# Four-layer trunk on one core: bank order and a fixed order in the convolution's end, the mean on VectorE, first q and k projected together

## The chip, the cores and the metric

The kernel runs on one core of one Trainium2 chip. The metric is the device time of one execution in microseconds; three executions of the kernel before took 1390.39, 1392.49 and 1392.76 us, median 1392.49. Times in the profile are microseconds from the start of the profiled span. Engines: PE is TensorE, PEld its loading of weights, DVE VectorE, ACT ScalarE, POOL GpSimd, SP the engine whose queue issues DMAs.

## The reference, cut to what matters

The input is one sequence of 256 frames with 1024 channels. Four layers follow each other, and each is x += mixer(rms_norm(x)), then x += squared-ReLU MLP(rms_norm(x)) with 4096 hidden channels. The mixers are retention (layers 0 and 3), a convolution module (layer 1) and stick-breaking attention (layer 2). All weights and activations are float32. The change touches these two mixers:

```python
def retention_mixer(xn, w_in, q_gain, k_gain, gn_w, gn_b, w_out):
    q, k, v, g = jnp.split(xn @ w_in, [D_MODEL, 2 * D_MODEL, 4 * D_MODEL], axis=-1)
    q = rms_norm(q.reshape(b, s, RET_HEADS, RET_DK), q_gain)     # 4 heads of 256
    k = rms_norm(k.reshape(b, s, RET_HEADS, RET_DK), k_gain)
    q = apply_rotary(q, s)
    k = apply_rotary(k, s) * (RET_DK ** -0.5)
    ...

def conformer_conv_mixer(xn, pw1_w, pw1_b, dw_w, dw_b, ln_w, ln_b, pw2_w, pw2_b):
    a, gate = jnp.split(xn @ pw1_w + pw1_b, 2, axis=-1)
    h = a * jax.nn.sigmoid(gate)
    h = causal_depthwise_conv(h, dw_w) + dw_b                    # 31 taps, 1024 channels
    h = layer_norm(h, ln_w, ln_b)                                # over the channels
    h = jax.nn.silu(h)
    return h @ pw2_w + pw2_b
```

## The kernel before

Activations lie channel-major: x is four tiles of 128 partitions by two blocks of 256 frames, and a block of 128 channels is called d or k (0 to 7). Products in float32 are made of rounded parts: an activation block z is a tile with a hi half and a lo half side by side (ACT writes hi, L417; DVE writes lo, L418), and each weight unit is split the same way.

**Weights.** 442 units of 128 x 1024 float32, in the order of a list (PLAN), two to a chunk of 1 MB, stream through three buffers (`raw`) by DMAs on SP's queue (L338). Each unit is cast by ACT to `wh` (L350) and DVE subtracts to get `wl` (L351); there are five buffers of each. The buffers `raw` are also used for the shifted copies of the convolution's input (L886).

**Projections.** There are two forms for a pair of 128-column blocks. The wide one (`pair_w`, matmuls at L497 and L498) multiplies `wh` by both halves of z in one matmul of 512 columns, and `wl` by the hi half in one of 256; it needs two PSUM banks, and afterwards the two halves of a bank are summed: two copies on ACT (L516) and two additions on DVE (L517). The narrow one (`pair_b`, L470 to L472) uses three matmuls of 256 columns, one bank, and nothing to sum. PSUM has four banks in the pool `acc` and four in the pool `mis`.

**Retention.** For each head, q and then k are projected with `pair_w`, squared by ACT, scaled, rotated on DVE (L695, L696, L698, L699), and POOL adds the squares of a head's two blocks to a tile. The squares are summed over channels by one matmul for each head on its own group of 32 columns (L704; the trace holds two records for each). The rms of x (`norm_r`) is made beside the first pair. Value projections follow (L857 to L859). At the program's start nine matmuls on ones (L295) keep PE busy while x and the first weights arrive; x, the parameters and pieces of 256 KB of weights alternate on SP's queue.

**Convolution.** Blocks 0 and 1 are convolved on DVE and on ACT with POOL, blocks 2 to 7 on PE by 64 records of small matmuls each (L966) from shifted copies of the input. The results of two blocks share one PSUM bank: 2 and 3, 4 and 5, 6 and 7. DVE takes each block out of PSUM, adding a bias and subtracting a shift (`fin_pe`, L1007), and ACT squares it (L975). Then a matmul adds blocks by column groups (`stats`, L981), four blocks to four groups; ACT copies the result (L1036), eight small matmuls make mean and mean square per frame (L387), DVE copies them (L1043), makes the variance and a reciprocal root by small operations on two columns (L371 to L382), and mean and root are broadcast over partitions by PE and ACT (L394, L398). POOL subtracts the mean from each block (L1054), DVE multiplies by the root (L1062), ACT applies the swish (L1063), and the result is split (L362, L363) for the second pointwise projection, which is 192 narrow matmuls into four banks. A few matmuls on ones (L295) fill PE's waits. DVE then adds the projection to x (L839) and writes the next z (L418) while POOL adds squares (L433).

**Order.** Everywhere but in marked places a scheduler that works when the program is built decides each engine's order. In the convolution the order is written by hand: each step gets a due time from the table TP, the steps are sorted by it, and instructions inside keep that order; weight splits come in between where the scheduler puts them.

## Time and profile before

| | |
|---|---|
| median of three executions | 1392.49 us |
| profiled execution, its own time | 1391.27 us |
| its span | 1389.5 us |
| mean granted TensorE clock | 0.994 |
| busy: PE, PEld, DVE, ACT, POOL | 98 %, 88 %, 71 %, 56 %, 10 % |
| TensorE busy, us | 1367.6 |

The page lists, for the whole span, how busy each engine was and the chain of work that ended last. A timeline row gives the start, the length, the engine, the line, the operation with its tiles, how many instructions were merged, and in brackets for how long the engine had been idle before and what ended that. A windows row gives the busy time of each engine in a stretch. The granted clock is 1.00 at 2.4 GHz and near 0.5 at 1.2 GHz.

### The profile page before, as it was taken

Reading aid. Unit: us, or ns where it says so; the run is one execution under the profiler, and the core shown is the slowest. Engines: PE = TensorE matmul, PEld = TensorE weight load, DVE = VectorE, ACT = ScalarE, POOL = GpSimd, SP = SyncE. Lnnn points to the kernel's source line nnn. Section 1 sums busy time; section 2 is a strip of 40 time slices with the busy share of each in tenths; the row PEclk is TensorE's granted clock in tenths of the full one; section 3 lists DMA queues with packets and bytes.
Section 4 is the critical chain, followed back from the end, with each engine's and each line's share of the span. In section 5 each row is a group of like instructions: output and inputs, shape, how many; then the busy total and the mean of one; then the engine's idle time right before and its main releaser. Section 6 shows DMA issues by size and latency. Waiting matters only on the chain.

```text
span 1389.5 us, 22352 instructions
## 1 busy us (share of the span) xinstructions
PE 1367.6 (98%) x8950; PEld 1218.2 (88%) x8950; DVE 984.6 (71%) x1656; ACT 775.2 (56%) x1165; POOL 145.7 (10%) x133
## 2 busy tenths in 40 slices
PE   8999999999999799999999999999999999999998
PEld 6889999888999388888988898888978999988888
DVE  7976778775678388766578587755587687788643
ACT  6655456664456267654468666644565554555432
POOL 3201003000228020000000010000110010100011
PEclk9999999999999999999999999999999999999999
DMA  7554445555554535555543345555444444555551
GB/s 275 197 179 148 156 152 202 186 189 182 182 183 119 183 122 189 197 189 182 184 180 122 124 168 193 182 189 199 173 167 171 163 148 157 182 183 183 193 191 39
DMA packets 38936, 239.92 MB, mean 173 GB/s; under 512 B 4272, under 2 KB 8752, under 8 KB 11184
## 3 DMA queue, kind: packets, MB, share of 16 engines
q1 hardware_dynamic: 38544, 237.97, 48.8%
q8 instruction: 70, 1.15, 0.3%
q10 hardware_dynamic: 288, 0.52, 0.1%
q14 instruction: 34, 0.28, 0.1%
HBM read 236.54 MB, written 1.93 MB: 172 GB/s over the span
## 4 chain that ended last, share of the span: by engine, by line
PE 95%; DMA 2%; DVE 1%; ACT 1%; issue 0%; SPq 0%; DVEq 0%; ACTq 0%
PE acc L497 33%; PE acc L498 17%; PE acc L470 9%; PE acc L472 9%; PE acc L471 9%; PE acc L857 4%; PE acc L858 4%; PE acc L859 4%; DMA raw<-in_w 2%; PE acc L966 1%; PE mis L387 1%; PE acc L486 1%; PE acc L484 1%; PE acc L485 1%; PE mis L394 1%; DVE wl L351 1%
## 5 line engine op out<-in xcount | busy, mean ns | idle before, releaser
L351 DVE TENSOR_TENSOR wl<-raw,wh 128x1024 fp32r<-128x1024 f32 (+1 forms) x442 | 552.5, 1252 | 299.9 <-ACT wh L350 295.1
L350 ACT CAST wh<-raw 128x1024 fp32r<-128x1024 f32 (+1 forms) x442 | 460.9, 1044 | 436.8 <-PE acc L497 212.1
L497 PE MATMUL acc<-z,wh 128*128 128x512 f32 x1248 | 438.9, 397 | 4.0 <-ACT wh L350 2.1
L498 PE MATMUL acc<-z,wl 128*128 128x256 f32 x1248 | 348.8, 282 | 0.3 <-DVE wl L351 0.3
L497 PEld LDWEIGHTS acc<-z,wh 128*128 128x128 f32 x1248 | 233.9, 189 | 60.5 <-ACT wh L350 3.5
L497 PE MATMUL acc<-big,wh 128*128 128x512 f32 x768 | 267.7, 393 | 0.0
L498 PEld LDWEIGHTS acc<-z,wl 128*128 128x128 f32 x1248 | 236.5, 190 | 3.2 <-DVE wl L351 1.8
L498 PE MATMUL acc<-big,wl 128*128 128x256 f32 x768 | 215.2, 280 | 0.0
L497 PEld LDWEIGHTS acc<-big,wh 128*128 128x128 f32 x768 | 143.8, 187 | 32.7
L472 PE MATMUL acc<-big,wl 128*128 128x256 f32 x576 | 162.3, 283 | 0.0
L471 PE MATMUL acc<-big,wh 128*128 128x256 f32 x576 | 162.3, 283 | 0.0
L470 PE MATMUL acc<-big,wh 128*128 128x256 f32 x576 | 161.5, 284 | 0.0
L498 PEld LDWEIGHTS acc<-big,wl 128*128 128x128 f32 x768 | 145.1, 189 | 0.0
L470 PE MATMUL acc<-z,wh 128*128 128x256 f32 x416 | 118.3, 285 | 0.0
L472 PE MATMUL acc<-z,wl 128*128 128x256 f32 x416 | 118.0, 284 | 0.0
L471 PE MATMUL acc<-z,wh 128*128 128x256 f32 x416 | 117.8, 284 | 0.0
L433 POOL TENSOR_TENSOR t<-t,t 128x512 f32<-128x512 f32 x25 | 38.8, 1554 | 735.1 <-DVE z L418 457.1
L470 PEld LDWEIGHTS acc<-big,wh 128*128 128x128 f32 x576 | 109.5, 192 | 1.3 <-DVE big L362 0.8
L471 PEld LDWEIGHTS acc<-big,wh 128*128 128x128 f32 x576 | 110.4, 192 | 0.1
L472 PEld LDWEIGHTS acc<-big,wl 128*128 128x128 f32 x576 | 110.4, 192 | 0.0
L516 ACT COPY t<-acc 128x256 f32<-128x256 f32 x180 | 65.2, 372 | 56.5 <-PE acc L498 56.5
L857 PE MATMUL acc<-wh,z 128*128 128x512 f32 x224 | 87.9, 394 | 0.0
(232 smaller groups left out, 1807.9 us busy)
## 6 DMA issues: line engine op xcount, KB each, us to landing
raw<-in_w SPq DMA_DIRECT2D x216, 1024.0 KB, 4.8
raw<-hd SPq DMA_DIRECT2D x12, 263.0 KB, 5.3
raw<-in_w SPq DMA_DIRECT2D x6, 512.0 KB, 7.6
x<-in_x SPq DMA_DIRECT2D x4, 256.0 KB, 6.1
raw<-in_w SPq DMA_DIRECT2D x4, 256.0 KB, 7.2
hd<-big SPq DMA_DIRECT2D x6, 143.5 KB, 3.0
cst<-in_cst SPq DMA_DIRECT2D x4, 192.0 KB, 5.0
cst<-in_cst SPq DMA_DIRECT2D x1, 548.0 KB, 8.8
```

The costliest lines, as they stand in the source:

```text
L350: nc.scalar.copy(hi[:, s], src[:, s])
L351: nc.vector.tensor_sub(lo[:, s], src[:, s], hi[:, s])
L433: (nc.vector if p == 3 and self.quick else nc.gpsimd).tensor_add(a, self.sq, q)
L470: nc.tensor.matmul(o, wh[:, kk, cs], ah, start=st, stop=False, **kw)
L471: nc.tensor.matmul(o, wh[:, kk, cs], al, start=False, stop=False, **kw)
L472: nc.tensor.matmul(o, wl[:, kk, cs], ah, start=False, stop=en, **kw)
L497: nc.tensor.matmul(ps[m], wh[:, kk, cs], a, start=first and kk == 0, stop=False, **kw)
L498: nc.tensor.matmul(ps[m][:, :S], wl[:, kk, cs], a[:, :S], start=False, stop=last and kk == 3, **kw)
L516: nc.scalar.copy(o[:, s], ps[m][:, S:])
L857: nc.tensor.matmul(ps[t], zh[:, s], wh[:, kk], start=k == 0, stop=False, skip_group_check=True)
L858: nc.tensor.matmul(ps[t], zh[:, s], wl[:, kk], start=False, stop=False, skip_group_check=True)
L859: nc.tensor.matmul(ps[t], zl[:, s], wh[:, kk], start=False, stop=k == 7, skip_group_check=True)
```

## The change

First layer: `PLAN` gets four units that hold q's and k's weights of the first head side by side, and `pairs_qk` uses two banks of `acc` and two of `mis`, so that each z is multiplied with both. The first weights come in pieces of 512 KB, x in between, and the first four units, not two, are split in halves. The other three heads of layer 0 use the narrow form; layer 3 keeps the wide one. The rms of x in layer 0 is made beside the third head. The four matmuls on the sums of squares are kept together, the last head's first, in both retention layers.

Convolution: blocks 2 to 7 take banks in turn, each bank's second half three blocks later. The due times go; the steps stand in a fixed order. Take-outs, stats, and weight splits are put in order by `issue_after`: the first two splits of the second projection after the take-out of block 5, the rest after the square of block 7 and the third y. The stats by column groups take blocks 0 to 5; blocks 6 and 7 are summed straight to columns. Mean and mean square are read from PSUM. The mean is subtracted on DVE, four blocks at a time, and the swish's input is written in place.

```diff
-                ps = self.pair_w("ret_w_in", j, isk * D + h * DK, self.zs)
+                if j == h == 0:
+                    if not isk:
+                        first = self.pairs_qk("ret_w_in", j, 0)
+                    ps = first[isk]
+                else:
+                    ps = (self.pair_w if j else self.pair_b)("ret_w_in", j, isk * D + h * DK, self.zs)
...
+    def pairs_qk(self, name, l, c0):
+        ps = [[self.acc(), self.acc()], [self.mis(), self.mis()]]
+        for kb in range(4):
+            w = self.unit((name, l, "qk", kb, c0))
+            wh, wl = v3(w[0], 2, 512), v3(w[1], 2, 512)
+            for kk, e in ((0, 0), (0, 1), (1, 0), (1, 1)) if kb < 3 else ((0, 0), (1, 0), (0, 1), (1, 1)):
+                k = kb * 2 + kk
+                z = self.zs(k)
+                for m in range(2):
+                    cs = slice(e * 256 + m * P, e * 256 + (m + 1) * P)
+                    o = ps[e][m]
+                    nc.tensor.matmul(o, wh[:, kk, cs], z, start=k == 0, stop=False, **kw)
+                    nc.tensor.matmul(o[:, :S], wl[:, kk, cs], z[:, :S], start=False, stop=k == 7, **kw)
+        return [self.sum_w(ps[0]), self.sum_w(ps[1])]
...
-        for h in range(RH):
-            nc.tensor.matmul(sr[32 * h : 32 * h + 32], self.c("o32", 32), sst[h], start=True, stop=True)
+        for h in (3, 0, 1, 2):
+            mm = nc.tensor.matmul(sr[32 * h : 32 * h + 32], self.c("o32", 32), sst[h], start=True, stop=True)
+            if h != 3:
+                self.tc.keep_in_program_order(mm)
...
-            pb[d] = pbs[i // 2][:, (i % 2) * S : (i % 2 + 1) * S]
+            pb[d] = pbs[i % 3][:, (i // 3) * S : (i // 3 + 1) * S]
...
+            taps_pe(4)
+            fin_pe(4)
+            taps_pe(5)
+            fin_pe(5)
+            stats(0, 1, 2, 3)
+            taps_pe(6)
+            fin_pe(6)
+            stats(4, 5)
+            sm, L["sc"] = self.tmp(), self.mis()
+            nc.scalar.copy(sm, L["st"])
+            taps_pe(7)
+            fin_pe(7)
+            cols(sm, 128, first=True)
+            cols(cc[6], 1024)
+            cols(cc[7], 1024, (0,))
+            cols(cc[7], 1024, (1,), last=True)
...
-        for d in range(8):
-            nc.gpsimd.tensor_sub(cc[d][:, :S], cc[d][:, :S], mb)
...
+            def swish(d):
+                c = cc[d][:, :S]
+                if d % 4 == 0:
+                    for e in range(d, d + 4):
+                        o = cc[e][:, :S]
+                        nc.vector.tensor_sub(o, o, mb)
+                nc.vector.tensor_mul(c, c, rsb)
...
+                if d == 2:
+                    after = [(L["sq", 4], L["fin", 5])] * 2 + [(L["sq", 7], self.last_lo)] * 14
```

PE at the program's start, first q and k of layer 0. `acc` and `mis` are PSUM banks, `z` the activation block, `wh` and `wl` the halves of a weight unit. Before:

```order
L497 MATMUL acc_150<-z_126,wh_152 128x512
L497 MATMUL acc_151<-z_126,wh_152 128x512
L498 MATMUL acc_150<-z_126,wl_153 128x256
L498 MATMUL acc_151<-z_126,wl_153 128x256
L497 MATMUL acc_150<-z_129,wh_152 128x512
L498 MATMUL acc_150<-z_129,wl_153 128x256
L497 MATMUL acc_151<-z_129,wh_152 128x512
L498 MATMUL acc_151<-z_129,wl_153 128x256
```

and in the changed kernel:

```order
L538 MATMUL acc_148<-z_124,wh_152 128x512
L538 MATMUL acc_149<-z_124,wh_152 128x512
L538 MATMUL mis_150<-z_124,wh_152 128x512
L538 MATMUL mis_151<-z_124,wh_152 128x512
L539 MATMUL acc_148<-z_124,wl_153 128x256
L539 MATMUL acc_149<-z_124,wl_153 128x256
L539 MATMUL mis_150<-z_124,wl_153 128x256
L539 MATMUL mis_151<-z_124,wl_153 128x256
```

Before, one z feeds the two banks of q; now it feeds the two banks of q and the two of k before the next z.

DVE at the convolution's end, from the take-out of block 2 (`big` from `acc`) on; `raw` to `wl` is a weight split of the second projection. Before:

```order
L1007 SCALAR_TENSOR_TENSOR big_4816<-acc_4826,prm,Gb_5024 128x256
L1007 SCALAR_TENSOR_TENSOR big_4817<-acc_4826,prm,Gb_5024 128x256
L1007 SCALAR_TENSOR_TENSOR big_4818<-acc_4827,prm,Gb_5024 128x256
L351 TENSOR_TENSOR wl_5303<-raw_5300,wh_5302 128x1024
L351 TENSOR_TENSOR wl_5331<-raw_5300,wh_5330 128x1024
L1007 SCALAR_TENSOR_TENSOR big_4819<-acc_4827,prm,Gb_5024 128x256
L351 TENSOR_TENSOR wl_5361<-raw_5358,wh_5360 128x1024
L351 TENSOR_TENSOR wl_5389<-raw_5358,wh_5388 128x1024
L1007 SCALAR_TENSOR_TENSOR big_4820<-acc_4828,prm,Gb_5024 128x256
L351 TENSOR_TENSOR wl_5419<-raw_5416,wh_5418 128x1024
L1007 SCALAR_TENSOR_TENSOR big_4821<-acc_4828,prm,Gb_5024 128x256
```

and in the changed kernel, whose L1045 is the same take-out:

```order
L1045 SCALAR_TENSOR_TENSOR big_4878<-acc_4888,prm,Gb_5086 128x256
L1045 SCALAR_TENSOR_TENSOR big_4879<-acc_4889,prm,Gb_5086 128x256
L1045 SCALAR_TENSOR_TENSOR big_4880<-acc_4890,prm,Gb_5086 128x256
L1045 SCALAR_TENSOR_TENSOR big_4881<-acc_4888,prm,Gb_5086 128x256
L351 TENSOR_TENSOR wl_5361<-raw_5358,wh_5360 128x1024
L351 TENSOR_TENSOR wl_5389<-raw_5358,wh_5388 128x1024
L1045 SCALAR_TENSOR_TENSOR big_4882<-acc_4889,prm,Gb_5086 128x256
L1045 SCALAR_TENSOR_TENSOR big_4883<-acc_4890,prm,Gb_5086 128x256
```

The take-outs of neighbouring blocks now read different banks, and of the five splits that stood ahead of block 7's take-out two are left, behind the first four take-outs and ahead of block 6's.

DVE at the end of the second projection, where the MLP of layer 1 begins. `x` is a pair of the residual, `z` its next activation block. Before:

```order
L839 SCALAR_TENSOR_TENSOR x_106<-acc_5296,prm,x_106 128x256 x2
L351 TENSOR_TENSOR wl_5603<-raw_5580,wh_5602 128x1024
L418 SCALAR_TENSOR_TENSOR z_5448<-x_106,prm_90,z_5448 128x256
L418 SCALAR_TENSOR_TENSOR z_5451<-x_106,prm_90,z_5451 128x256
L839 SCALAR_TENSOR_TENSOR x_110<-acc_5297,prm,x_110 128x256 x2
L351 TENSOR_TENSOR wl_5642<-raw_5639,wh_5641 128x1024
L418 SCALAR_TENSOR_TENSOR z_5486<-x_110,prm_90,z_5486 128x256
L418 SCALAR_TENSOR_TENSOR z_5489<-x_110,prm_90,z_5489 128x256
L839 SCALAR_TENSOR_TENSOR x_113<-acc_5298,prm,x_113 128x256 x2
```

and in the changed kernel, whose L868 is the addition of L839:

```order
L868 SCALAR_TENSOR_TENSOR x_107<-acc_5354,prm,x_107 128x256 x2
L868 SCALAR_TENSOR_TENSOR x_111<-acc_5355,prm,x_111 128x256 x2
L351 TENSOR_TENSOR wl_5661<-raw_5638,wh_5660 128x1024
L868 SCALAR_TENSOR_TENSOR x_114<-acc_5356,prm,x_114 128x256 x2
L351 TENSOR_TENSOR wl_5700<-raw_5697,wh_5699 128x1024
L418 SCALAR_TENSOR_TENSOR z_5506<-x_107,prm_90,z_5506 128x256
L868 SCALAR_TENSOR_TENSOR x_117<-acc_5357,prm,x_117 128x256 x2
L418 SCALAR_TENSOR_TENSOR z_5509<-x_107,prm_90,z_5509 128x256
L351 TENSOR_TENSOR wl_5720<-raw_5697,wh_5719 128x1024
L418 SCALAR_TENSOR_TENSOR z_5544<-x_111,prm_90,z_5544 128x256
L418 SCALAR_TENSOR_TENSOR z_5547<-x_111,prm_90,z_5547 128x256
L351 TENSOR_TENSOR wl_5778<-raw_5775,wh_5777 128x1024
```

Before, each pair's addition is followed by its own two z; now three pairs are added before the first z, and the fourth before the second.

## Rows read from the trace of the kernel before

**Rows 1.** The page, chain that ended last, share of the span by engine
```profile
PE 95%; DMA 2%; DVE 1%; ACT 1%; issue 0%; SPq 0%; DVEq 0%; ACTq 0%
```

**Rows 2.** Windows: stretch, us, busy us of each engine, PEclk, DMA, GB/s
```profile
0.00:30.00 30.00, 24.35 (x113) 17.57 (x114) 20.24 (x31) 19.95 (x33) 8.81 (x10) 1.00 0.78 274
...
440.00:512.00 72.00, 61.78 (x654) 43.52 (x653) 38.08 (x75) 29.11 (x49) 12.64 (x17) 0.93 0.51 156
```

**Rows 3.** Windows of PE alone: stretch, us, busy, PEclk, DMA, GB/s
```profile
30.10:33.40 3.30, 3.30 (x13) 0.52 0.80 322
470.50:477.10 6.60, 2.80 (x28) 0.51 0.58 209
...
491.00:514.00 23.00, 23.00 (x190) 1.00 0.39 137
```

**Rows 4.** Timeline, last taps of layer 1: start, us, engine [idle before]
```profile
458.09 3.24 PE L966 MATMUL acc<-raw,big 128*32 128x256 f32 x56 [0.61 <-DVE big L1007]
...
462.07 2.00 ACT L350 CAST wh<-raw 128x1024 fp32r<-128x1024 f32 x2 [5.46 <-DMA raw<-in_w]
463.15 2.36 DVE L351 TENSOR_TENSOR wl<-raw,wh 128x1024 fp32r<-128x1024 f32 x2 [5.11 <-ACT wh L350]
...
470.42 1.99 ACT L350 CAST wh<-raw 128x1024 fp32r<-128x1024 f32 x2 [4.06 <-DMA raw<-in_w]
471.49 2.36 DVE L351 TENSOR_TENSOR wl<-raw,wh 128x1024 fp32r<-128x1024 f32 x2 [5.59 <-ACT wh L350]
...
473.77 0.48 DVE L1007 SCALAR_TENSOR_TENSOR big<-acc,prm,Gb 128x256 f32<-128x256 f32 x1
...
474.30 4.74 PE L966 MATMUL acc<-raw,big 128*32 128x256 f32 x56 [6.42 <-DVE big L1007]
...
479.12 0.48 DVE L1007 SCALAR_TENSOR_TENSOR big<-acc,prm,Gb 128x256 f32<-128x256 f32 x1 [3.74 <-PE acc L966]
```

**Rows 5.** Timeline, from the take-out of block 7 to the second projection
```profile
481.19 0.59 ACT L1036 COPY t<-mis 128x512 f32<-128x512 f32 x1 [1.13 <-PE mis L981]
...
484.36 0.16 DVE L378 SCALAR_TENSOR_TENSOR vy<-vt,vy 128x2 f32<-128x2 f32 x1
484.53 5.86 POOL L1054 TENSOR_TENSOR big<-big,lnb 128x256 f32<-128x256 f32 x8 [29.80 <-DVE vy L378]
...
485.31 0.65 DVE L381 SCALAR_TENSOR_TENSOR vt<-vt,lnm 128x2 f32<-128x2 f32 x1
...
487.97 2.70 DVE L1062 TENSOR_TENSOR t<-big,lnr 128x256 f32<-128x256 f32 x3 [1.34 <-ACT lnr L398]
...
490.80 0.41 DVE L1062 TENSOR_TENSOR t<-big,lnr 128x256 f32<-128x256 f32 x1
...
490.94 0.78 PE L470 MATMUL acc<-big,wh 128*128 128x256 f32 x4
```

**Rows 6.** Timeline of DVE, start of the MLP of layer 1
```profile
514.62 1.91 DVE L418 SCALAR_TENSOR_TENSOR z<-x,prm,z 128x256 fp32r<-128x256 f32 x2
```

**Rows 7.** Timeline of PE, first q and k of layer 0
```profile
6.64 1.22 PE L497 MATMUL acc<-z,wh 128*128 128x512 f32 x2 [1.32 <-ACT wh L350]
...
19.05 0.40 PE L497 MATMUL acc<-z,wh 128*128 128x512 f32 x1
...
19.39 0.40 PE L497 MATMUL acc<-z,wh 128*128 128x512 f32 x1
...
29.25 0.50 PE L497 MATMUL acc<-z,wh 128*128 128x512 f32 x1 [1.96 <-DVE t L517]
```

**Rows 8.** Timeline of DVE, splits ahead of the sum that PE waits for
```profile
20.02 5.96 DVE L351 TENSOR_TENSOR wl<-raw,wh 128x1024 fp32r<-128x1024 f32 x3 [1.18 <-ACT wh L350]
```

**Rows 9.** Timeline of PE, sums of squares in layers 0 and 3
```profile
54.00 1.05 PE L704 MATMUL mis<-big,cst 128*32 128x512 f32 x4
54.98 0.50 PE L497 MATMUL acc<-z,wh 128*128 128x512 f32 x1
...
1021.58 1.04 PE L704 MATMUL mis<-big,cst 128*32 128x512 f32 x2
```

More of the change, by code (lines that the diff above doesn't have):

```diff
@@ L68, in _plan @@
             for h in range(RH):
+                if i == h == 0:
+                    u += [("ret_w_in", j, "qk", kb, 0) for kb in range(4)]
+                    continue
                 u += _b_pair("ret_w_in", j, h * DK, 2)
@@ L346, in unit @@
         lo = self.wp.tile([P, 1024], F32R, name=self.nm("wl"), tag="wl")
-        n = 512 if self.un < UPC else 1024
-        for i in range(0, 1024, n):
-            s = slice(i, i + n)
-            nc.scalar.copy(hi[:, s], src[:, s])
-            nc.vector.tensor_sub(lo[:, s], src[:, s], hi[:, s])
+        n = 512 if self.un < 2 * UPC else 1024
+        with ExitStack() as stack:
+            for i in after or ():
+                stack.enter_context(self.tc.issue_after(i.ins))
+            for i in range(0, 1024, n):
+                s = slice(i, i + n)
+                nc.scalar.copy(hi[:, s], src[:, s])
+                nc.vector.tensor_sub(lo[:, s], src[:, s], hi[:, s])
         self.un += 1
@@ L824, in retention, with out_proj @@
         self.out_proj("ret_w_out", j, y, 4, 2, nxt)
-    def out_proj(self, name, l, y, nkb, group, nxt, bias=None, before=None):
+    def out_proj(self, name, l, y, nkb, group, nxt, bias=None, before=None, after=None):
         nc = self.nc
@@ L843, in evac @@
             self.norm_pair(p, *nxt)
-        self.res_pairs(name, l, acts, nkb, group, evac, before)
+        self.res_pairs(name, l, acts, nkb, group, evac, before, after)
     def mm_a(self, ps, w, kb):
@@ L962, in tap_pool, with taps_pe @@
                 nc.gpsimd.tensor_add(a, a, pr)
-        def taps_pe(d, g):
-            for j in range(4):
+        def taps_pe(d):
+            for g, j in ((g, j) for g in range(NG) for j in range(4)):
                 nc.tensor.matmul(
@@ L969, in taps_pe, with stats, cols @@
                 )
-        L = {"n": 0}
+        L = {}
         def square(d):
-            nc.scalar.activation(out=cc[d][:, S:], in_=cc[d][:, :S], func=AF.Square)
-        def stats(d):
-            n = L["n"]
-            L["n"] += 1
-            o = 32 * (n % 4)
-            nc.tensor.matmul(L["st"][o : o + 32], self.c("o32", 32), cc[d], start=n < 4, stop=n > 3, **kw)
+            L["sq", d] = nc.scalar.activation(out=cc[d][:, S:], in_=cc[d][:, :S], func=AF.Square)
+        def stats(*ds):
+            for d in ds:
+                o = 32 * (d % 4)
+                nc.tensor.matmul(L["st"][o : o + 32], self.c("o32", 32), cc[d], start=d < 4, stop=d in (2, 3, 4, 5), **kw)
+        def cols(src, sc, es=(0, 1), first=False, last=False):
+            for e in es:
+                for t in range(2):
+                    i = t * 2 + e
+                    self.colsum(
+                        L["sc"][:, i : i + 1], src[:, e * S + t * P : e * S + (t + 1) * P], self.sc(sc),
+                        first and i == 0, last,
+                    )
         def sum_1():
@@ L1068, in stick @@
+        self.out_proj("conv_pw2_w", j, y, 2, 4, nxt, bias="pw2b", after=after)
     def stick(self, j, nxt):
```

124 lines of the change are left out of this document (53 added, 71 removed).

## Prediction

> **What bounds the kernel now.** The page's chain comes first: of the span that ends last, 95 % runs through PE, 2 % through DMA, 1 % each through DVE and ACT [rows 1]. So a microsecond counts only if it is PE work removed, or PE idle or slow-running time removed. I therefore asked the windows view for the stretches that the diff touches. In the first 30 us PE is busy 24.35; in the convolution's end, 440 to 512 us, it is busy 61.78 of 72 at a mean granted clock of 0.93 [rows 2]. Elsewhere the diff changes nothing that PE waits for, so these two stretches, and the summing matmuls of the two retention layers, are all there is to win. The clock view says that PE runs at 0.51 to 0.52 of full speed (the 1.2 GHz level) in short stretches just after it has waited, and at 1.00 through the second pointwise projection [rows 3]. The timelines then tell who was waited for.
>
> **The convolution's end, part by part.** Six channel blocks (d = 2 to 7) have their taps summed by PE, two blocks to a PSUM bank. PE waits 0.61 us before the taps of block 5 and 6.42 us before those of block 7, each time for a take-out (L1007) on DVE from the bank that it shares with the block before [rows 4]. The long one has a history: ACT waits for a weight DMA (4.06), casts, DVE waits for the cast (5.59), splits two units (2.36), and only then reaches the take-out of block 6 that stands behind them in DVE's order; it ends at 474.25 and PE goes on at 474.30 [rows 4]. The change removes both halves: blocks 5 to 7 share banks with blocks 2 to 4, taken out long before, and in the new order only the first two splits stand ahead of a take-out of block 6.
>
> - The two waits: -7.0. The taps of block 7 then no longer begin at half clock: 2.80 us of PE work at 0.51 becomes 1.4 [rows 3], another -1.4. Two things remain on this path: one pair of splits (2.36 us, started at 463.15 [rows 4], so over by 465.5, about when block 6's taps end) and the two summing matmuls of blocks 4 and 5, so I give 0.2 back and count **-8.2**.
> - The sums of blocks 6 and 7 go straight to columns. What leaves the path is ACT's wait of 1.13 for the four-block sum, its copy of 0.59, and the copy of mean and square to SBUF, 0.16 as small DVE operations go; **-1.9** [rows 5].
> - The mean is subtracted on DVE. While POOL subtracts (5.86 us for eight), DVE's operations on two columns take 0.65 where they are alone 0.16, and the multiplications 0.90 (2.70 for three) where one alone takes 0.41 [rows 5]. Three such small ones and one multiplication are on the path: -1.5 and -0.5. The subtractions come back on DVE: four before the first multiplication, 4 x 0.41 = 1.64, of which some 1.2 lies under the broadcast of the reciprocal root; +0.4. Sum **-1.6**. The other four, 1.64 us, stand ahead of weight splits and halves of y; PE's 192 matmuls of the projection take 23 us [rows 3], so most is hidden, and I give one stall of **+0.4**. Were that cover gone, it would be 1.6.
>
> So the projection starts 8.2 + 1.9 + 1.6 = 11.7 us earlier, and ends 11.3 earlier. Not all of that reaches the end. Before, the residual additions, splits and lo halves of z alternate on DVE at the projection's end, and the MLP starts at once. In the new order x of the first three pairs is done, and a split, before the first z. I followed DVE's rows with the durations of before (a split 1.2 [rows 4], a lo half 0.41 to 0.96): the eighth z is ready an estimated 9 to 10 us after the projection. Two pairs of the MLP use the same z, four steps of 0.35 each, so PE can fill 7 x 1.4 = 9.8 us before it needs the eighth, but the early z come late as well. I take **+2.4** (ends 0.5 and 6). A lo half beside POOL's square sums takes 0.96 (1.91 for two [rows 6]) and not 0.41; that is why the upper end is so far.
>
> Two shorter low-clock stretches may come with such stalls. The nearest priced one is 3.3 us at 0.52 [rows 3], which costs 1.6; I take **+1.0** (0 to 3). Convolution: -11.7 + 0.4 + 2.4 + 1.0 = **-7.9** (ends -13 and -3.5).
>
> The Trainium skill ("SBUF — State Buffer", Who interferes with whom) says that a DVE instruction with two SBUF inputs and a GpSimd instruction that reads SBUF exclude each other for a whole instruction. The trace agrees in direction [rows 5]; by the rule, the same lock would meet the six lo halves that now stand in a row beside POOL's square sums, which speaks against this change and for the upper end of the 2.4.
>
> **The start.** The first head's q and k now use each arriving z together: eight matmuls for each z and not four, over twice the weights.
>
> - First two pairs. Before, PE waits 1.32 us for the first cast of weights that are still arriving (the DMA engines are 78 % busy) [rows 2, 7]. They now need the same four units, in two pieces of 512 KB and then more; 32 steps of 0.35 [rows 7] are 11.2 us whichever order they have. The first matmul comes later (twice the piece, 0.9 us at 274 GB/s [rows 2]) and later ones wait less. I take **-0.8** (ends +0.5 and -1.6).
> - The other six q and k pairs of layer 0 use three narrow matmuls per step and not a wide and a narrow one. 48 x 0.121 (190 in 23 us [rows 3]) is 5.8 us where 16 x 0.35 is 5.6; six times 0.2 is **+1.2**. The narrow form needs one accumulator bank, not two, and no summing.
> - That summing is what PE waits for at 29.25: 1.96 us, for an accumulator whose sum on DVE stands behind three splits (5.96 us), two rotations and a fourth split [rows 7, 8]. With one bank per pair and nothing to sum, the wait goes, and with it the 3.3 us at 0.52 that follow it [rows 3]: -1.96 - 1.6 = **-3.6** (ends -1.5 and -3.6). Next late there are the splits: DVE had 20.24 of 30 us busy and keeps that, plus the last sums of the first pairs; I give **+0.6** (0 to 2).
> - Layer 0's sums of squares, four matmul pairs on four column groups: before in three places, each costing PE 0.98 whether it holds two heads (54.00, next at 54.98) or one [rows 9]; two column groups in one place already run at the same time. In one place they cost one stop, so 2 x 0.98 = **-1.9**.
>
> Start: -0.8 + 1.2 - 3.6 + 0.6 - 1.9 = **-4.5** (ends -2 and -8).
>
> **Layer 3.** The same matmuls stood in four places there (one is shown [rows 9]; the others are alike); in one place three stops go: **-2.9** (ends -1.5, if four groups together take two stops' time, and -3.1). They stand behind the first value projection, long after the last head's squares, so I see nothing that they wait for.
>
> **Sum.** -7.9 - 4.5 - 2.9 = -15.3 on the profiled execution's 1391.27 us: 1376.0. The median of the three runs is 1.2 above that execution, so 1377.2; its own spread is 2.4. I say **1376.5**, between the two.
>
> **The rivals.**
>
> - *DVE takes the place of the bank.* The eight subtractions, five splits and the late z make DVE the engine that PE waits for, from the projection's start into the MLP. For it: the new DVE order has z behind additions and splits. Against: DVE is busy 38.08 of 72 us there [rows 2]. Price: the +2.4 becomes 6 and the +0.4 becomes 1.6, +1.0 becomes 3: 1383. Chance 0.15.
> - *The wait moves on and the order does not do what it says.* Block 6's take-out still stands behind two splits, whose weights landed only at 462.07 [rows 4]. If the DMA of these weights lands 5 us later than before, since it stands behind the strips of the last blocks, the 6.42 comes back in part: about 1381. For it: ACT waited 5.46 for this very landing. Against: nothing in front of it was added. Chance 0.08.
> - *The start does not move*, because weights and not summing set it, and the wait of 1.96 comes back as one for a split: +4, 1380.5. For it: the DMA share of 0.78. Against: in the row at 29.25 the weights had long been split. Chance 0.10.
> - *Slower: the clock.* PE is used sparsely from block 7's end to the projection's first matmuls, and it fell to 0.51 after a wait in this very place. If the low level stays through the projection, whose 23 us at 1.00 [rows 3] become 46, the sum turns to +8, about 1400. It decides as soon as 15 us of PE time more run at the low level. Against: in before the low stretch at 470.5 ended after 6.6 us, and the matmuls that only keep PE busy are all still there. Chance 0.03. Beside it, the Trainium skill ("TensorE: Matmul & The Clock Gate", HAM oscillation) describes kernels that fall back after every wait; the two low stretches shown after waits agree that it happens, none of them repeats itself without a new wait.
> - *All gains, no giving back*: the MLP starts without stall and no low stretch is left, 1376.5 - 3.4 - 0.5 - 1.1 = about 1371. Chance 0.09.
>
> **How the numbers follow.** The forecast (1373 to 1380) keeps 0.55. The range of 8 in 10 reaches over the four faster cases and leaves out the ends: sums of the lower and upper ends give -24 and -7, that is 1368.5 and 1385.5; I leave a little off each: **1368.5 to 1384.5**. The measurement of this kernel tells about 0.2 %, 2.8 us, from no change. Only the clock case ends above; for several givebacks at once I leave 0.03 to "same". Faster 0.94, same 0.03, slower 0.03.
>
> **What would show it.** In the changed kernel's profile: no PE wait for a take-out in the taps, block 7's taps beginning near 466 less what the start gained; the second projection's first matmul some 16 us earlier than 490.94 [rows 5] (11.7 and the start's 4.5); the four sum matmuls in one row of about 1 us each in layers 0 and 3; no PE wait for a sum near 29 us; PE waits for z at the MLP's start of layer 1. I am wrong if PE waits there for more than 6 us, if the low clock lasts into the projection, or if the first value projection of layer 0 does not start 2 to 7 us earlier than before.

## The result, and the profile after

The changed kernel takes 1374.02 us (median of four executions, 1373.77 to 1374.17), the kernel before 1392.01 beside it; the ratio is 0.9872, 95 % interval 0.9855 to 0.9889. That is 18 us faster; 1376.5 was predicted, within 1368.5 to 1384.5. The span fell from 1389.5 to 1372.0.

The page's chain, to be set beside [rows 1], has a point less of DMA and a point more each of PE and DVE:

```profile
PE 96%; DVE 2%; DMA 1%; ACT 1%; issue 0%; SPq 0%; POOL 0%; ACTq 0%; DVEq 0%; POOLq 0%
```

The windows view of the same two stretches, engines in the order PE, PEld, DVE, ACT, POOL, then PEclk, DMA share and GB/s ([rows 2]; the second stretch now lies earlier, and covers 77 us):

```profile
0.00:30.00 30.00, 26.95 (x166) 22.32 (x167) 19.54 (x31) 22.50 (x39) 7.62 (x10) 1.00 0.84 307
...
423.00:500.00 77.00, 73.43 (x780) 60.23 (x780) 49.45 (x99) 37.70 (x68) 17.66 (x20) 0.98 0.56 162
```

PE is busy 26.95 of the first 30 us where it was busy 24.35, and at a mean clock of 0.98 in the convolution's end, not 0.93.

The timeline of PE from the start ([rows 7, 9] before):

```profile
6.43 0.74 PE L538 MATMUL acc<-z,wh 128*128 128x512 f32 x2 [1.13 <-ACT wh L350]
...
18.08 0.28 PE L470 MATMUL acc<-z,wh 128*128 128x256 f32 x1
...
19.03 0.38 PE L472 MATMUL acc<-z,wl 128*128 128x256 f32 x1 [0.55 <-DVE wl L351]
...
42.06 0.60 PE L387 MATMUL mis<-cst,t 128*128 128x1 f32 x4 [0.83 <-POOL t L441]
...
66.64 1.06 PE L731 MATMUL mis<-big,cst 128*32 128x512 f32 x8
...
1035.01 1.06 PE L731 MATMUL mis<-big,cst 128*32 128x512 f32 x8
```

The first matmul begins as early as before (6.43, before 6.64), but q and k of the first head are done at 18.08; the wait of 1.96 us for a sum is gone; a small wait of 0.55 for a split is there, and a new one of 0.83 for GpSimd at 42 us. L731 (before L704) is one row of eight records in each retention layer: four heads in 1.06 us. The taps of layer 1 begin at 438.6, 6.4 us earlier than before.

The timeline of all engines in the convolution's end ([rows 4, 5] before; L995 are the taps, L1045 the take-outs, L1100 the subtraction of the mean, L1101 the multiplication by the root):

```profile
457.46 2.36 DVE L351 TENSOR_TENSOR wl<-raw,wh 128x1024 fp32r<-128x1024 f32 x2 [2.75 <-ACT wh L350]
...
459.37 3.88 PE L995 MATMUL acc<-raw,big 128*32 128x256 f32 x59
459.74 0.48 DVE L1045 SCALAR_TENSOR_TENSOR big<-acc,prm,Gb 128x256 f32<-128x256 f32 x1
...
463.32 0.48 DVE L1045 SCALAR_TENSOR_TENSOR big<-acc,prm,Gb 128x256 f32<-128x256 f32 x1 [3.11 <-PE acc L995]
...
466.06 0.16 DVE L1084 COPY lnc<-mis 128x2 f32<-128x2 f32 x1 [2.25 <-PE mis L387]
...
467.62 0.16 DVE L380 TENSOR_TENSOR vt<-vy 128x2 f32<-128x2 f32 x1
...
468.16 1.43 DVE L1100 TENSOR_TENSOR big<-big,lnb 128x256 f32<-128x256 f32 x4
...
469.95 0.76 DVE L1101 TENSOR_TENSOR big<-big,lnr 128x256 f32<-128x256 f32 x2 [0.36 <-ACT lnr L398]
...
471.39 0.74 PE L470 MATMUL acc<-big,wh 128*128 128x256 f32 x4
```

No tap matmul waits. Block 7's taps run (the last 59 of them from 459.37) while block 6's take-out (459.74) has not yet begun, block 7's own take-out comes at 463.32 (before 479.12), mean and square are there at 466.06, the small operations take 0.16 (before 0.65 beside GpSimd), and the second projection starts at 471.39 (before 490.94).

What is given back stands in the timeline of PE behind that:

```profile
477.04 0.39 PE L472 MATMUL acc<-big,wl 128*128 128x256 f32 x1 [0.58 <-DVE wl L351]
...
497.97 0.50 PE L497 MATMUL acc<-z,wh 128*128 128x512 f32 x1 [2.44 <-DVE z L418]
...
500.00 0.50 PE L497 MATMUL acc<-z,wh 128*128 128x512 f32 x1 [0.35 <-DVE z L418]
...
502.55 0.50 PE L497 MATMUL acc<-z,wh 128*128 128x512 f32 x1 [0.88 <-DVE z L418]
```

and in VectorE's at the same place (L868 adds to x, L351 splits weights, L418 makes the lo halves of z):

```profile
492.82 1.66 DVE L868 SCALAR_TENSOR_TENSOR x<-acc,prm,x 128x256 f32<-128x256 f32 x4 [3.43 <-PE acc L472]
494.39 1.22 DVE L351 TENSOR_TENSOR wl<-raw,wh 128x1024 fp32r<-128x1024 f32 x1
...
497.44 0.48 DVE L418 SCALAR_TENSOR_TENSOR z<-x,prm,z 128x256 fp32r<-128x256 f32 x1
...
498.62 1.32 DVE L418 SCALAR_TENSOR_TENSOR z<-x,prm,z 128x256 fp32r<-128x256 f32 x1
...
501.00 2.93 DVE L418 SCALAR_TENSOR_TENSOR z<-x,prm,z 128x256 fp32r<-128x256 f32 x2
...
505.53 1.66 DVE L418 SCALAR_TENSOR_TENSOR z<-x,prm,z 128x256 fp32r<-128x256 f32 x4
```

VectorE adds two pairs, splits, adds, splits, and makes the first z at 497.44; beside GpSimd's sums the next lo halves take 1.32 and 2.93 (two), and the last four 0.42 each. PE waits 2.44, 0.35 and 0.88 us here, and 0.41 once more behind that: 4.1 in all.

### The profile page after: what moved, and what is told of

It is laid out like the page before. It is cut to its first block, busy times and chain, and to the rows that moved or that the text cites. A ratio compares the mean times of both kernels' runs of the same rounds, so it can differ in the third digit from the quotient of the medians.

```text
span 1372.0 us, 22537 instructions
## 1 busy us (share of the span) xinstructions
PE 1357.4 (99%) x9057; PEld 1224.0 (89%) x9058; DVE 978.4 (71%) x1653; ACT 770.9 (56%) x1155; POOL 136.0 (10%) x125
## 4 chain that ended last, share of the span: by engine, by line
PE 96%; DVE 2%; DMA 1%; ACT 1%; issue 0%; SPq 0%; POOL 0%; ACTq 0%; DVEq 0%; POOLq 0%
PE acc L497 32%; PE acc L498 16%; PE acc L472 9%; PE acc L470 9%; PE acc L471 9%; PE acc L887 4%; PE acc L886 4%; PE acc L888 4%; PE acc L995 2%; PE mis L387 1%; DMA raw<-in_w 1%; PE mis L394 1%; DVE wl L351 1%; PE acc L486 1%; PE acc L484 1%; PE acc L485 1%
## 5 line engine op out<-in xcount | busy, mean ns | idle before, releaser
L351 DVE TENSOR_TENSOR wl<-raw,wh 128x1024 fp32r<-128x1024 f32 (+1 forms) x444 | 552.1, 1247 | 283.2 <-ACT wh L350 278.1
L497 PE MATMUL acc<-z,wh 128*128 128x512 f32 x1120 | 391.8, 395 | 4.1 <-DVE z L418 4.1
L498 PE MATMUL acc<-z,wl 128*128 128x256 f32 x1120 | 312.6, 281 | 0.0
L497 PEld LDWEIGHTS acc<-z,wh 128*128 128x128 f32 x1120 | 209.2, 187 | 52.3 <-DVE z L418 5.2
L498 PEld LDWEIGHTS acc<-z,wl 128*128 128x128 f32 x1120 | 211.6, 189 | 1.0
L472 PE MATMUL acc<-z,wl 128*128 128x256 f32 x512 | 145.2, 284 | 0.5 <-DVE wl L351 0.5
L470 PE MATMUL acc<-z,wh 128*128 128x256 f32 x512 | 145.4, 284 | 0.0
L471 PE MATMUL acc<-z,wh 128*128 128x256 f32 x512 | 144.9, 283 | 0.0
L472 PEld LDWEIGHTS acc<-z,wl 128*128 128x128 f32 x512 | 98.1, 192 | 0.8 <-DVE wl L351 0.8
L471 PEld LDWEIGHTS acc<-z,wh 128*128 128x128 f32 x512 | 98.1, 192 | 0.0
```

The source lines that it names most:

```text
L351: nc.vector.tensor_sub(lo[:, s], src[:, s], hi[:, s])
L470: nc.tensor.matmul(o, wh[:, kk, cs], ah, start=st, stop=False, **kw)
L471: nc.tensor.matmul(o, wh[:, kk, cs], al, start=False, stop=False, **kw)
L472: nc.tensor.matmul(o, wl[:, kk, cs], ah, start=False, stop=en, **kw)
L497: nc.tensor.matmul(ps[m], wh[:, kk, cs], a, start=first and kk == 0, stop=False, **kw)
L498: nc.tensor.matmul(ps[m][:, :S], wl[:, kk, cs], a[:, :S], start=False, stop=last and kk == 3, **kw)
```

## The experiments

### Each part alone

Three kernels, each with one part of the change on the kernel before. The sums of squares:

```diff
-        for h in range(RH):
-            nc.tensor.matmul(sr[32 * h : 32 * h + 32], self.c("o32", 32), sst[h], start=True, stop=True)
+        for h in (3, 0, 1, 2):
+            mm = nc.tensor.matmul(sr[32 * h : 32 * h + 32], self.c("o32", 32), sst[h], start=True, stop=True)
+            if h != 3:
+                self.tc.keep_in_program_order(mm)
```

> The kernel before with one edit: in both retention layers the four matmuls on the sums of squares stand together, the last head's first. Theory: each place costs TensorE one stop of 0.98 us whether it holds one head or two, so two stops go in layer 0 and three in layer 3: -4.9 us, about 1387. Rival 1: four column groups together take the time of two stops: -2.9, about 1389. Rival 2: they were hidden, or the first of them now waits for the last head's squares: no change, 1392. In the trace the theory wants one row of four heads of about 1 us in each of the two layers, with no wait ahead of it.

1385.34 us, ratio 0.9960 (0.9948 to 0.9973): -5.6 us. The timeline of PE in this kernel, layer 0, has the row

```profile
71.06 1.06 PE L704 MATMUL mis<-big,cst 128*32 128x512 f32 x8
```

four heads in the time that one took ([rows 9]). The stop is a price for each place, not for each head; the theory holds. The price is higher than the 0.98 of the theory, though: in layer 3 the stretch from the rms broadcast to the first value projection holds the same projection matmuls and takes 21.11 us with three stops (from 1020.57 in the kernel before) and 17.55 with none (from 1018.41 here), so 1.19 for a stop, and 5.9 for five.

The start (first q and k together, first DMAs, narrow pairs, rms of x later), with the sums and the convolution of before:

```diff
+                    u += [("ret_w_in", j, "qk", kb, 0) for kb in range(4)]
...
+                        first = self.pairs_qk("ret_w_in", j, 0)
...
+                    ps = (self.pair_w if j else self.pair_b)("ret_w_in", j, isk * D + h * DK, self.zs)
...
+                if (h, isk) == ((0, 0) if j else (2, 0)):
```

> The changed kernel with the convolution's part and the sums of squares as before: only the first head's q and k together, the new order of the first DMAs, the narrow form for the other six pairs of layer 0, and the rms of x beside the third head. Theory: the convolution of layer 1 began 6.4 us earlier in the changed kernel, and 1.95 of that are two stops of the sums, so this one gives -4.4 us, about 1387.6. Rival: the parts help each other (without the sums together the wait for a sum is still there in another place), and this part alone gives -2 or less, 1390. In the trace: no TensorE wait of 1.96 near 29 us and no low clock at 30 us.

1386.42 us, ratio 0.9972 (0.9961 to 0.9983): -4.5 us. No wait for a sum near 29 us.

The convolution, with start and sums of before:

```diff
+            pb[d] = pbs[i % 3][:, (i // 3) * S : (i // 3 + 1) * S]
...
+            taps_pe(6)
+            fin_pe(6)
+            stats(4, 5)
...
+            taps_pe(7)
+            fin_pe(7)
...
+        self.out_proj("conv_pw2_w", j, y, 2, 4, nxt, bias="pw2b", after=after)
```

> The kernel before with the convolution's part alone: banks in turn, fixed order, splits pinned, blocks 6 and 7 summed to columns, mean on VectorE. Theory: between the first tap matmul and the second projection's first matmul the changed kernel is 13.2 us shorter, and gives back 0.6 in the projection and 4.1 at the MLP's start; alone it gives -8.3, about 1383.7, and the three parts (-4.9, -4.4, -8.3) add up to the whole. Rival: the waits at the MLP's start come from the DMAs' phase after a shorter start and are not there when the start is as before: -12, 1380.

1383.94 us, ratio 0.9950 (0.9938 to 0.9962): -7.0 us. It has the same 4.1 us of waits for z at the MLP's start, so these belong to the convolution's part and not to the phase of the DMAs. It falls 1.3 us short of its forecast, which had counted idle time alone: from the second projection's first matmul to the first one of the MLP's second product it takes 119.2 us for 113.1, so 6.1 are given back and not 4.7.

The three sum to -17.0 us. The whole change gave -18.0, and -17.6 when it was run again on another chip, each time against the kernel before beside it. So the parts add up to the whole within about 1 us, which is no more than the spread of one kernel's executions.

### Banks without the order, order without the banks

```diff
-            pb[d] = pbs[i // 2][:, (i % 2) * S : (i % 2 + 1) * S]
+            pb[d] = pbs[i % 3][:, (i // 3) * S : (i // 3 + 1) * S]
```

This line on the kernel before, whose order on every engine stays:

> The kernel before with one line changed: blocks 2 to 7 take PSUM banks in turn; every engine's order is that of before. Theory: bank and order hold about half each. The taps of block 7 no longer wait for block 6's take-out (6.42 us), but the take-outs of blocks 6 and 7 still stand behind weight splits on VectorE, so the take-out of block 7 moves only from 479.1 to about 475.4 and the time by -3.7 to -4.5: about 1388. Rival 1: the bank is everything, -7 to -8.5, 1384. Rival 2: the order is everything and the wait only moves: 0, 1392.

1388.87 us, ratio 0.9984 (0.9975 to 0.9993): -2.0 us, less than any of the theories that gave it something. The timeline of all engines:

```profile
466.63 4.04 PE L966 MATMUL acc<-raw,big 128*32 128x256 f32 x58
...
473.53 0.48 DVE L1007 SCALAR_TENSOR_TENSOR big<-acc,prm,Gb 128x256 f32<-128x256 f32 x1
...
474.51 3.44 PE L981 MATMUL mis<-big,cst 128*32 128x512 f32 x4 [3.84 <-ACT big L975]
475.06 0.48 DVE L1007 SCALAR_TENSOR_TENSOR big<-acc,prm,Gb 128x256 f32<-128x256 f32 x1
...
487.60 0.74 PE L470 MATMUL acc<-big,wh 128*128 128x256 f32 x4 [1.88 <-DVE big L362]
```

and the window of PE from there to the projection:

```profile
476.00:488.00 12.00, 9.45 (x35) 0.69 0.36 150
```

The wait of 6.42 before block 7's taps is gone, and block 7's take-out is at 475.06, as expected. But now PE waits 3.84 us for the square of block 6, whose take-out still stands behind the splits at 473.53, and it runs at 0.69 of full clock up to the projection. The wait moved from the taps to the sums. The projection starts 3.3 us earlier than before, and 2.6 of these are lost in it again (the MLP's first matmul comes 0.8 us earlier, 513.5 for 514.3). Some 1.7 of the 2.6 are a stretch at half clock inside the projection (granted clock 0.50 from 490.2 to 493.6); this profiled execution is the longest of eleven (1390.49), and whether the others have that stretch the runs don't tell.

The other way round, the changed kernel with the sharing of before:

```diff
-            pb[d] = pbs[i % 3][:, (i // 3) * S : (i // 3 + 1) * S]
+            pb[d] = pbs[i // 2][:, (i % 2) * S : (i % 2 + 1) * S]
```

> The changed kernel with blocks 2 and 3, 4 and 5, 6 and 7 again in one PSUM bank each; the fixed order stays. Theory: with the fixed order the sharing costs only what the take-out of the block before lasts: about 0.6 us before block 5 and 1.5 before block 7 (its taps began at 458.8, block 6's take-out ended at 460.2), perhaps a short stretch at half clock: +2 to +3, about 1376.5. Rival: the bank is what matters and the order is worth little: +7, 1381. Another: nothing, because the stats matmuls cover it: 1374.

1374.77 us, ratio 0.9892 (0.9878 to 0.9905), 0.7 us above the changed kernel run again on another chip (1374.10, of which more below). Against the kernel before beside each, it saves 16.1 us and the changed kernel 17.6, which makes the difference 1.5. The timeline of all engines:

```profile
454.24 3.68 PE L995 MATMUL acc<-raw,big 128*32 128x256 f32 x64 [0.61 <-DVE big L1045]
...
460.33 2.36 DVE L351 TENSOR_TENSOR wl<-raw,wh 128x1024 fp32r<-128x1024 f32 x2 [1.86 <-ACT wh L350]
...
462.61 0.47 DVE L1045 SCALAR_TENSOR_TENSOR big<-acc,prm,Gb 128x256 f32<-128x256 f32 x1
...
463.14 3.67 PE L995 MATMUL acc<-raw,big 128*32 128x256 f32 x64
```

0.61 us before block 5, as forecast, and none before block 7: the take-out of block 6 comes at 462.61, right behind the two splits, and the taps go on at 463.14, since the summing matmuls of blocks 4 and 5 fill the time. (This profiled execution took 1378.64 and is the longest of four; its start is 3 us late, of which more below.) So with the order fixed the turn of banks is worth 1 us or so, little more than the noise. The order, together with the sums to columns and the mean on VectorE that stay in this kernel, carries the rest; the order alone was not run. Of the two halves that the prediction took together, one was worth little.

### The mean on GpSimd

The changed kernel with one engine's name changed:

```diff
-                        nc.vector.tensor_sub(o, o, mb)
+                        nc.gpsimd.tensor_sub(o, o, mb)
```

> The changed kernel with the eight subtractions of the mean on GpSimd again, in the same places of the program. Theory: VectorE's three small operations of the root take 0.65 and not 0.16 beside GpSimd, and the first multiplication waits: the second projection begins 1 to 2 us later, and the time is +1 to +2, about 1375.5. Rival: what VectorE loses there it gets back, since 3.3 us of subtractions leave it ahead of the weight splits and of the MLP's z; the waits of 4.1 at the MLP's start shrink by 2 to 3, and the time is -1 to -2, about 1372.5.

1374.74 us, ratio 0.9885 (0.9870 to 0.9901), 0.6 above the changed kernel of the other chip; against the kernel before beside each the difference is 1.5. The timeline of all engines:

```profile
467.22 5.87 POOL L1100 TENSOR_TENSOR big<-big,lnb 128x256 f32<-128x256 f32 x8 [18.63 <-DVE vt L377]
...
467.99 0.65 DVE L381 SCALAR_TENSOR_TENSOR vt<-vt,lnm 128x2 f32<-128x2 f32 x1
...
470.66 1.84 DVE L1101 TENSOR_TENSOR big<-big,lnr 128x256 f32<-128x256 f32 x2 [1.34 <-ACT lnr L398]
...
473.29 0.74 PE L470 MATMUL acc<-big,wh 128*128 128x256 f32 x4 [1.20 <-DVE big L362]
```

Both theories are half right. The small operations take 0.65 again and two multiplications 1.84 instead of 0.76; from the first tap to the projection's first matmul it is 34.4 us for 32.8 (-1.6 had been the term). But the way from there to the MLP is 25.5 us for 26.6: VectorE, 3.3 us of subtractions lighter, is 1.1 us less late with y and z. Net the mean on VectorE is worth about 1 us, between 0.6 and 1.5 by what it is set against, and no more than the noise.

### Wide pairs in layer 0

```diff
-                    ps = (self.pair_w if j else self.pair_b)("ret_w_in", j, isk * D + h * DK, self.zs)
+                    ps = self.pair_w("ret_w_in", j, isk * D + h * DK, self.zs)
```

> The changed kernel with the wide form (two banks and a sum) for the other six q and k pairs of layer 0. Theory: the wait for a sum on VectorE comes back, 1 to 2 us and a low clock of up to 1.6 behind it, against 6 x 0.2 us of TensorE saved: +0.5 to +2.4, about 1375.5. Rival: the new start alone had removed the wait, and the narrow form only costs: -1.2, about 1372.8.

1381.43 us, ratio 0.9938 (0.9925 to 0.9950): 7.3 us slower than the changed kernel, outside both forecasts. The timelines of VectorE and of PE:

```profile
24.58 5.98 DVE L351 TENSOR_TENSOR wl<-raw,wh 128x1024 fp32r<-128x1024 f32 x3 [1.84 <-ACT wh L350]
...
37.50 0.74 DVE L521 TENSOR_TENSOR t<-acc,t 128x256 f32<-128x256 f32 x2
...
38.05 0.76 PE L497 MATMUL acc<-z,wh 128*128 128x512 f32 x1 [7.86 <-DVE t L521]
```

and PE's window behind it:

```profile
39.50:42.00 2.50, 2.50 (x9) 0.50 0.02 8
```

With two banks for each pair the third and the fourth pair hold all four banks of `acc`. The fifth waits 7.86 us for the sum of the third, which stands at 37.50 behind rotations and six splits on VectorE, and then PE runs at half clock for some five microseconds. The sum: 7.9 of wait and some 2.5 of low clock, less the 1.2 that the narrow form costs and the waits of 0.83 and 0.55 that are not met here, is 7.8 for 7.3 measured (the profiled execution begins the first value projection 8.3 us later than the changed kernel's). The new start gained 6.4 us in the changed kernel; with the wide form nothing of that would be left.

### The MLP's start: VectorE's order pinned

```diff
+                        if p:
+                            stack.enter_context(self.tc.issue_after(self.zlo[2 * p - 1].ins))
...
+        for n, d in ((1, 3), (2, 3), (3, 7)):
+            self.pin[self.un + n] = [self.zlo[d]]
```

> The changed kernel with VectorE's order at the MLP's start of layer 1 pinned: each pair's addition to x comes after the two z of the pair before, and the second to fourth weight split of the MLP after the fourth, fourth and eighth z. Theory: the four TensorE waits there (4.1 us in all) come from z standing behind additions and splits; in this order the early z are ready before the projection ends, one wait of about 0.7 for the second pair's weights stays, and the time is -3, about 1371. Rival: the four accumulators of the projection finish too close together (within 3.5 us), so whatever stands first the last z or the weight splits are late: -1 or less, 1373 to 1374.5.

1380.49 us, ratio 0.9927 (0.9914 to 0.9940): 6.4 us slower than the changed kernel. The theory fell. VectorE's timeline and the PE row that followed:

```profile
501.56 0.88 DVE L420 SCALAR_TENSOR_TENSOR z<-x,prm,z 128x256 fp32r<-128x256 f32 x2 [1.54 <-ACT z L419]
```

```profile
507.16 0.39 PE L500 MATMUL acc<-z,wl 128*128 128x256 f32 x1 [3.16 <-DVE wl L353]
```

Pinned in that order, each pair's z waits for ScalarE's hi half, which waits for the addition just before (1.54 us idle here). The early z are ready sooner, as the theory had it: from the projection's first matmul to the MLP's first it is 23.5 us for 26.6. But PE then waits 3.16 us for one of the splits that were moved back, and from the projection's end it waits 5.2 us in all, 1.1 us more than without the pins.

That does not make 6.4 us. From the projection's first matmul to the end the profiled execution is 3.2 us longer than the changed kernel's, and most of that is no wait: PE is busy without a gap in the MLP and still gets through fewer matmuls. Its window in the changed kernel, then in this one:

```profile
540.00:640.00 100.00, 100.00 (x579) 1.00 0.54 190
```

```profile
540.00:640.00 100.00, 100.00 (x568) 1.00 0.52 189
```

A step of two matmuls takes 353 ns there, and 347 in the same MLP of every other kernel of this document, which makes some 2.6 us over the layer. Why the pins slow the steps stays open. The other 4 us of this execution lie ahead of the projection: a start that is 3 us later, and a stretch at a granted clock of 0.50 (from 468.0 to 474.8, longer than the changed kernel's), with which it takes 1 us more from the first tap to the projection. Whether all five executions had those the runs don't tell, so of the 6.4 us 3.2 are shown to come with the pins.

### The MLP's start: without GpSimd beside z

The four squares of x and their sums are traced after the MLP's first pair:

```diff
-            self.norm_pair(p, *nxt)
+            self.norm_pair(p, *nxt, sq=bias is None)
...
+            if self.sq is None and p == 0:
+                for q in range(4):
+                    self.norm_sq(q)
```

> The changed kernel itself once more, as the yardstick for the three that run beside it on the same chip: 1374 by its first runs, if the chip behaves alike.

> The changed kernel with one edit: the squares of x of layer 1's MLP, four on ScalarE and their three sums on GpSimd, are traced after the MLP's first pair and not between the z. Theory: VectorE's lo halves of z take 1.32 and 2.93 (two) beside GpSimd's sums where they take 0.42 to 0.48 alone, so that VectorE is 2.8 us late with the eighth z; without GpSimd beside them TensorE's waits of 4.1 us at the MLP's start fall to about 2, and the time is -2, 1372. Rival: the waits come from additions and weight splits standing ahead of z, which stay as they are: -0.5 or less.

The changed kernel, measured beside it, took 1374.10 (ratio 0.9874); this one 1372.18 (0.9860, 0.9845 to 0.9874): -1.9 us, and from the projection's first matmul to the first one of the MLP's second product 117.1 us for 119.0. VectorE's timeline:

```profile
502.54 0.87 DVE L418 SCALAR_TENSOR_TENSOR z<-x,prm,z 128x256 fp32r<-128x256 f32 x2
...
504.47 1.66 DVE L418 SCALAR_TENSOR_TENSOR z<-x,prm,z 128x256 fp32r<-128x256 f32 x4
```

Every lo half takes 0.42 to 0.48, also the third and fourth that took 2.93 together, and PE's waits here are the 2.44 alone; 0.35 and 0.88 are gone. The Trainium skill ("SBUF — State Buffer", Who interferes with whom) says that a VectorE instruction with two SBUF inputs and a GpSimd instruction that reads SBUF shut each other out; the runs agree, with 1.32 to 1.47 beside GpSimd and 0.42 without, and show that it reached the end of the chain. The remaining 2.44 are the additions and splits ahead of the first z.

### The new wait at 42 us

In layer 0 the rms of x now ends in a GpSimd sum that is placed beside the third head. The timeline of GpSimd in the changed kernel shows what it waited for:

```profile
40.44 1.57 POOL L441 TENSOR_TENSOR t<-t 128x256 f32<-128x256 f32 x1 [3.10 <-DVE big L726]
```

L726 is a step of a head's rotation, which has nothing to do with x: the sum's new buffer is one that VectorE still reads. Written in place it needs none:

```diff
-            sq, n = self.tmp(S), 1
+            sq, n = self.sq[:, :S] if inplace else self.tmp(S), 1
...
-                    self.norm_r()
+                    self.norm_r(inplace=not j)
```

> The changed kernel with one edit: in layer 0 the last sum for the rms of x is written by GpSimd over its own input and not into a new buffer. Theory: in the changed kernel this sum waits 3.10 us for a buffer that VectorE still reads (rotation of the second head), and TensorE waits 0.83 us for it at 42 us, or 1.6 us and then 3.3 us at half clock in those executions in which the first matmuls run at half clock. In place it waits for nothing: no TensorE wait there, -0.8 us, and the executions that are 3 to 4 us longer are gone. Rival: the wait is for GpSimd's other work, or moves to the next step of the same chain: no change.

1372.59 us, ratio 0.9860 (0.9845 to 0.9875), -1.5 beside the changed kernel, whose profiled execution waited 1.58 us here this time; the first value projection begins at 54.2 for 55.7. PE's row for the sum, without a wait:

```profile
36.45 0.50 PE L387 MATMUL mis<-cst,t 128*128 128x1 f32 x4
```

The four executions lie within 0.7 us (1372.07 to 1372.80), those of the changed kernel beside it within 2.4.

Both edits together:

> The two edits together (the rms sum of layer 0 in place, the squares of layer 1's MLP later). If both theories hold: -2.8, about 1371; if they do not disturb each other the sum of the two.

1371.82 us (1370.45 to 1372.17), ratio 0.9856 (0.9839 to 0.9872): -2.3 of the -3.4 that the two give apart, 20 us faster than the kernel before, and the best version here. Its profiled execution has both gains in full, and it settles the theory's second half: the first matmuls run at half clock in it (1.22 for two), and still the first value projection begins at 54.7, against 57.8 in the profiled execution of the kernel above with the squares later, which begins at half clock too and still has the wait for the rms. So the long executions come from that wait and what follows it, and the edit removes both.

## Why the prediction was right, step by step

Each step is set against the profiled executions, before and after.

- *Waits of the taps and the half clock there, -8.2.* From the first tap to the last it is 24.2 us for 33.7: -9.4. Right, and the mechanism too, but for the share of the banks: it is the order that took the wait away (1 us or so for the banks).
- *Sums to columns, -1.9, and mean on VectorE, -1.6.* From the last tap to the projection 8.5 us for 12.3: -3.8, against -3.5. The columns were not run alone. The projection started 13.2 us earlier, counted from the first tap, where 11.7 were forecast.
- *Given back, +0.4, +2.4 and +1.0.* PE's idle time is 0.58 in the projection and 4.1 at the MLP's start, together 4.7 for 3.8. From the projection's first matmul to the first one of the MLP's second product it is 119.0 us for 113.1, so 5.9 in all, 1.2 more than the idle time alone. The place and the mechanism were right (the first z behind additions and splits, and lo halves beside GpSimd, at 1.32 to 1.47 each where 0.96 was forecast); the size of the second was a little over half of the truth. In this execution the low clock did not come with these stalls. It came earlier, just behind the column sums:

```profile
465.20:468.40 3.20, 2.99 (x16) 0.62 0.69 282
...
471.00:497.00 26.00, 23.96 (x195) 1.00 0.36 125
```

  The second row here is the projection: 1.00 throughout. The rival of a clock that stays low did not happen. But that the stalls went without low clock was this execution's luck: in the profiled ones of the kernels with the rms sum in place and with the mean on GpSimd the granted clock is 0.50 right behind the same first wait for z (from 496.8 to 500.2, and from 498.9 to 502.4).
- *The start, -4.5.* It came out at -6.4. The first two pairs were the mis-sized term: done at 18.08 for 21.16, -3.1 instead of -0.8, because two pairs' work on each z fills the waits for the next one, and in this execution the first matmuls already ran at full clock (0.74 for two, 1.22 before). The second reason is luck: the execution with shared banks and the fixed order began at half clock, and its PE rows for the first matmuls and for the third pair are

```profile
6.82 1.22 PE L538 MATMUL acc<-z,wh 128*128 128x512 f32 x2 [1.50 <-ACT wh L350]
...
19.49 0.28 PE L470 MATMUL acc<-z,wh 128*128 128x256 f32 x1
```

  So at the clock of before the term is -1.7, about its stated end of -1.6. The old start did not gain from a full clock: the three kernels that keep it (sums alone, convolution alone, banks alone) took 0.73 for their first two matmuls and are done with two pairs at 20.6 to 21.8. The new DMA pieces and the pairing were not run apart. From there to the end of the last pair it is 36.9 us for 39.6, -2.7, and the four terms for that stretch (+1.2, -3.6, +0.6, and one stop of 0.98) sum to -2.8. The rest, -0.6, is the stop that goes from the first value projection, less a broadcast of the rms that now stands there. That no wait of 1.96 came back was right for the reason given, and the wide form shows how much hung on it: 7.86. What was not foreseen is the wait of 0.83 for the rms.
- *Layer 3, -2.9.* The four heads are one row of 1.06 us there. From the first q of the layer to the projection behind its mixing it is 99.1 us for 102.7: -3.6, beyond the stated end of -3.1, and the sums alone gave -5.6 for the 4.9 of both layers. The mechanism was right and the price of a stop too small, 0.98 for 1.19.

Of the rivals, the one of VectorE as the new bound was right in its place and small in its price: PE waits there 4.1 us. The weights of the first two splits landed as early relative to the taps as before (the splits run from 457.46, 18.8 us after the first tap; before 18.2), so that wait did not move. The sum, -15.3, is 2.2 us short of the -17.5 between the two profiled executions: 1.9 more from the start, 1.5 more from the convolution up to the projection and 0.9 more behind the MLP's first product, most of it layer 3's stops, against 2.1 more given back. So the path and the waits were foreseen, and that the total came so close is in part luck, because misses of about 2 us each cancelled. The start owes some 3 us to the clock as well: in the execution that began at half clock the first value projection comes at 57.9, 3.8 us earlier than before (61.7) and not 6.7.

## What to carry to other kernels

When an engine waits for a take-out from PSUM, look first at what stands ahead of the take-out on its own engine; another bank alone only moves the wait to the next reader. A form of a projection that needs no sum and one bank is worth its extra matmuls where the sum's engine has a backlog. And ask of each buffer that a side computation takes from a rotating pool who still reads its last content, and which engine's reads it will run beside.

## What the runs showed of the hardware

The first matmuls on real data ran at full clock in some executions and at half in others of nearly the same program: two took 0.74 us from 6.43 in the changed kernel, 1.22 from 6.82 where only the banks were shared as before, although the nine matmuls on ones ahead of them were the same. The execution with 1.22 had the wait for the rms at 1.63 and not 0.83, a granted clock of 0.50 after it, and began the value projection 2.9 us later (57.9 for 55.0). The longer wait is not enough for that: the changed kernel's second profiled execution began at full clock (0.73), waited 1.58 there, kept a granted clock of 1.00 after it and began the value projection at 55.7. The Trainium skill ("TensorE: Matmul & The Clock Gate", What's actually happening) says that the moment at which the clock rises varies from run to run; these rows agree. What sets it here stayed open.

Four matmuls on four groups of 32 columns took 1.06 us together, one took 1.04 ([rows 9]); set between other matmuls, such a place cost 1.19 us from start to start.
